# Earlier row gathers, stored up-products spread over all groups, and gates asked for mid-group in a product-key expert block

## The chip, the core and the metric

The kernel runs on one core of one Trainium2 chip. TensorE (PE) multiplies matrices into PSUM, VectorE (DVE) and ScalarE (ACT) work on SBUF and PSUM, GpSimd (POOL) issues the indirect gathers, SyncE (SP) issues most plain transfers, and 16 DMA engines carry out what all of them issue. The metric is the device time of one execution in microseconds.

## What is computed

One residual block on 512 tokens of width 2048, all in float32:

```
x = x + mixer(rms_norm(x))        # 8 stick-breaking and 8 forgetting heads, gated, projected
h = rms_norm(x)
x = x + peer_ffn(h)
out = rms_norm(x)

peer_ffn, for each token:
    for each of 8 heads: two 256-wide half queries score 128 sub-keys each,
        the best 16 of both sides are combined, and the best 16 of the 256 sums
        name 16 of 16384 experts, with softmax gates
    act  = gelu(dot(u[expert], h))             # 128 chosen experts a token
    out += gate * act * v[expert]
```

## The kernel before, in words

Every float32 operand of a matrix product is split into a rounded part and a rest, and a product is three matmuls (`mm3`, lines 115 to 118). `wload` (line 95) fetches a block of weights of 128 x 2048 in two halves of 512 KB through SP into `wr` (four buffers once `more` is set), ACT writes the rounded half `wh` (line 108) and DVE the rest `wl` (line 109). A block is 48 matmuls; in the expert part these have 352 columns.

**Two ways to the experts.** The first 352 tokens (`TD`) are computed densely: for each block c of 128 experts, of `NK` = 128 blocks, `expert_up(c)` multiplies by `uT[c]`, scales by `rstd` on DVE (line 536) and applies gelu on ACT; the product is multiplied by the gates of the block (zero where the token has not chosen the expert) and then by the block's rows of `vP`. The other 160 tokens (128 and 32) are done by gathering their rows: a queue `todo` of 325 items holds 128 + 32 gathers from `expert_u` and 128 + 32 from `expert_v` (one indirect DMA of 128 rows of 8 KB each on POOL, line 561, and one pass of DVE over 128 x 2048, lines 568, 577, 586, 597), and five entries for the changes of stage, two of them empty. `pace(after, units)` adds `units * rate[0]` to a counter and issues one item for each whole unit, its DVE pass placed behind the instruction `after`.

**The stages of the second half.** (1) Query: sixteen projections `wload(w_q[b])` with 512 columns, and after each pair `choose(h, ...)` for the last 256 tokens, some 70 small DVE instructions. After all heads one instruction writes `idx`, the 128 chosen rows of each of the last 128 tokens (line 741). (2) Early: `choose` for the first 256 tokens, and after each head `early(UPS, pace)`, which computes five up-products and stores them in DRAM (`gact_sp`); then 22 steps (line 777) that write the gates of 16 tokens each to DRAM (`gsp`), with further up-products in between. In all `NS` = 54 up-products are stored. The rate is `SLOW` = 0.8 items for each up-product. (3) The loop over 16 groups of `GC` = 8 blocks. `weigh(n)` makes sure that block n + 1 (`LEAD` = 1) is there too, by `fetch`: a stored product is read back (`gl<-gact_sp`, 176 KB, line 802), any other is computed. At the first block of a group it asks for the gates of the whole group in three transfers (`h<-gsp`, lines 812 to 815, pieces of 512 bytes, into one buffer `gg` in the unused columns of `h2`), multiplies (line 817), and splits into `wg` (lines 820 and 821). There are four buffers `gl` and nine `wg`. With the group's eight `wg` in place, eight blocks of `vP` are multiplied into `psy` and added to `acc` (line 841). An up-product and a `vP` block are one unit of the pace each; on entry to the loop the rate becomes the items left over 2 * 128 - 54 - 8 = 194.

In the kernel before, the stored products are blocks 0 to 53, so groups 0 to 5 and most of group 6 compute no up-product in the loop, and the later groups compute all eight. The order on each engine is laid out by a planner when the program is built, from program order, readiness and its own estimate of times; each engine then runs its list in order, waiting where data are not there.

Of the kernel before, what the change touches and what calls it, by code (L numbers as in the profile page):

```python
# [13 lines left out]
ALU = mybir.AluOpType  # L14
# [6 lines left out]
NT = T // P  # L21
D = 2048
KC = D // P
HD = 128
NH = 8
NK = 128
TOPK = 16
HK = NH * TOPK
# [3 lines left out]
GC = 8  # L32
NG = NK // GC
JJ = D // (GC * P)
TB = 16
# [3 lines left out]
TD = T - P - MB  # L39
# [2 lines left out]
CW = 112  # L42
UPS = 5
NS = NH * UPS + TD // TB - -(-(TD // TB) // 3)
SLOW = 0.8
LEAD = 1
NP = 4
# [3 lines left out]
def block_kernel(ctx, tc, xT, gains, w_vf, bf, w_qk, w_v, w_g, w_br, w_o, w_q, keysT, uT, vP, expert_u, expert_v, outT):  # L51
    nc = tc.nc
# [39 lines left out]

    WC = D // 2 + 4 * NH

    def wload(src, between=None, pace=None):

        out = []
        n = src.shape[-1] // 2
        for s in range(2):
            turn[0] += 1  # L100
            rp = more[0] if more and turn[0] % 2 else wp
            raw = rp.tile([P, WC], F32, tag="wr", name="wr", bufs=2)[:, :n]
            nc.sync.dma_start(raw, src[:, s * n:(s + 1) * n])
            if between and s == 0:
                between()
            hi = wp.tile([P, WC], F32R, tag="wh", bufs=3, name="wh")[:, :n]
            lo = wp.tile([P, WC], F32R, tag="wl", bufs=3, name="wl")[:, :n]
            nc.scalar.activation(hi, raw, AF.Copy)  # L108
            ins = nc.vector.tensor_tensor(lo, raw, hi.bitcast(F32), op=ALU.subtract)  # L109
            out.append((hi, lo))  # L110
            if pace and s == 0:
                pace(ins, 0.5)
        return out

    def mm3(ps, wh, wl, ah, al, start, stop):
        nc.tensor.matmul(ps, wh, ah, start=start, stop=False)  # L116
        nc.tensor.matmul(ps, wh, al, start=False, stop=False)  # L117
        nc.tensor.matmul(ps, wl, ah, start=False, stop=stop)  # L118

    def proj(ps, w, a, nk=KC, off=0, n=T):  # L120
        for k in range(nk):
            b = off + k
            wh, wl = w[b // 8]
            c = slice(b % 8 * P, (b % 8 + 1) * P)
            mm3(ps, wh[:, c], wl[:, c], a[:, k, 0, :n], a[:, k, 1, :n], k == 0, k == nk - 1)
# [12 lines left out]
    with ExitStack() as s1:  # L138
# [3 lines left out]
        with ExitStack() as s2:  # L142
# [16 lines left out]

            xload(0, 1)  # L160
            firstw = wload(w_qk[0, 0, 0], lambda: xload(1, 1))
            for k in range(2, KC, 2):
                xload(k, 2)
            for k in range(KC):
# [3 lines left out]
                                               op1=ALU.subtract)  # L168
# [252 lines left out]
            ps = pa.tile([P, NT, NH], F32, tag="z1", name="psc")  # L421
# [5 lines left out]
            ps = pa.tile([P, T], F32, tag="z0", name="pscT")  # L427
# [34 lines left out]
        h2 = h2p.tile([P, KC, 2, T], F32R, name="h2")  # L462
        with ExitStack() as s2:
# [7 lines left out]
            for j in range(KC):  # L471
                ps = pp.tile([P, T], F32, tag="pp", name="pso")
# [5 lines left out]
                                               op1=ALU.subtract)  # L478
# [8 lines left out]
    gsp = dram.tile([P, TD // TB, NK, TB], F32, name="gsp")  # L487
# [6 lines left out]
    idx = gpool.tile([P, HK], U32, name="idx")  # L494
# [37 lines left out]
    def expert_up(c, pace=None):  # L532
        ps = pu.tile([P, T], F32, tag="pu", name="psu")
        proj(ps[:, :TD], wload(uT[c], pace=pace), h2, n=TD)
        g = gl.tile([P, TD], F32, tag="gl", name="gl")
        ins = nc.vector.tensor_tensor(g, ps[:, :TD], rstd[:, :TD], op=ALU.mult)  # L536
        if pace:
            pace(ins, 0.5)
        nc.scalar.activation(g, g, AF.Gelu_apprx_tanh)
        return g  # L540
# [3 lines left out]
    gg = h2.rearrange("p k s t -> p (k s) t")[:, :TD // TB, TD:TD + GC * TB].bitcast(F32)  # L544
    gg = gg.rearrange("p b (c t) -> p b c t", t=TB)
# [3 lines left out]
    def pace(after, units):  # L549

        slot[0] += units * rate[0]
        while todo and slot[0] >= 1:
            f, i = todo.pop(0)
            f(i, after.ins)
            slot[0] -= 1
# [57 lines left out]
    todo = [(gather_up, i) for i in range(HK)] + [(lambda i, after: None, 0), (rows_b, 0)]  # L613
    todo += [(gather_up_b, i) for i in range(SB)] + [(gather_down, i) for i in range(HK)]
    todo += [(gather_down_b, i) for i in range(SB)] + [(lambda i, after: None, 0), (back, 0), (back_b, 0)]
    rate = [SLOW]

    gact_sp = dram.tile([NS, P, TD], F32, name="gact_sp")
    started = []

    def early(n, pace=None):
        for _ in range(n):
            if len(started) < NS:
                c = len(started)
                nc.scalar.dma_start(gact_sp[c], expert_up(c, pace))
                started.append(c)

    with ExitStack() as s1:
# [6 lines left out]
        ia = s1p.tile([P, NT, HK], F32, name="ia")  # L635
        ib = s1p.tile([P, NT, HK], F32, name="ib")
# [77 lines left out]
                                    op=ALU.mult)  # L714


        for h in range(NH):
            sc = []
            sv = se.tile([P, 2, HT, NK], F32, tag="sv", name="sv")
            for p in range(2):  # L720
                b = 2 * h + p
                if b == 1:
                    norm2()
                if b == 3:
                    token_rows(lambda k: acc[:, k, T - P:], h2g, accg)
                ps = pu.tile([P, T], F32, tag="pu", name="psq2")
                proj(ps, wload(w_q[b]), h2)
                q = se.tile([P, T], F32, tag="ab1", name="q2")
                nc.scalar.activation(q, ps, AF.Copy)
                kt = se.tile([P, NK], F32, tag="kt", name="kt")  # L730
                nc.sync.dma_start(kt, keysT[b])
                ps = psx.tile([P, NT, NK], F32, tag="psx", name="pss")
                for t in range(NT):
                    nc.tensor.matmul(ps[:, t], q[:, t * P:(t + 1) * P], kt, start=True, stop=True)
                nc.scalar.activation(sv[:, p], ps[:, :HT], AF.Copy)
                sc.append(ps[:, HT:])
            nc.scalar.dma_start(scores[h], sv)
            choose(h, sc, HT, NT - HT)


        nc.vector.scalar_tensor_tensor(idx, ia[:, NT - 1], float(NK), ib[:, NT - 1], op0=ALU.mult, op1=ALU.add)
        nc.vector.tensor_copy(ggate, gt[:, NT - 1])
        rep = se.tile([P, 2 * HK + 2], F32, tag="ab1", name="rep")
        nc.vector.scalar_tensor_tensor(rep[:, :HK], ia[:, NT - 2], float(NK), ib[:, NT - 2], op0=ALU.mult, op1=ALU.add)
# [4 lines left out]
        ps = psx.tile([P, T], F32, tag="psx", name="psrep")  # L749
# [18 lines left out]
        for n, src in enumerate((ia, ib, gt)):  # L768
            ps = psx.tile([P, ND, P], F32, tag="psx", name="pstr")
# [7 lines left out]
        for tb in range(TD // TB):  # L777
            st = se.tile([P, NK, TB], F32, tag="st", name="st")
            for t4 in range(0, TB, 4):
# [4 lines left out]
                ps = pg.tile([P, 4, NK], F32, tag="pg", name="psgt")  # L784
                for i in range(4):
                    t = tb * TB + t4 + i
                    nc.vector.tensor_scalar(ab[0][:, i], i128, tr[0][:, t:t + 1], tr[2][:, t:t + 1], op0=ALU.is_equal,  # L787
                                            op1=ALU.mult)
# [7 lines left out]
    extra.append(ex)  # L796

    def fetch(c):
        if c >= NS:
            return expert_up(c, pace)  # L800
        g = gl.tile([P, TD], F32, tag="gl", name="gl")
        nc.sync.dma_start(g, gact_sp[c])
        return g


    ahead = []

    def weigh(n):

        while len(ahead) < min(n + 1 + LEAD, NK):  # L810
            ahead.append(fetch(len(ahead)))
        if n % GC == 0:
            for b in range(0, TD // TB, 8):
                e = min(b + 8, TD // TB)
                nc.sync.dma_start(gg[:, b:e], gsp[:, b:e, n:n + GC])
        g = ahead[n]
        nc.vector.tensor_tensor(g.rearrange("p (b t) -> p b t", t=TB), g.rearrange("p (b t) -> p b t", t=TB),
                                gg[:, :, n % GC], op=ALU.mult)
        wg = ex.tile([P, 2, TD], F32R, tag="wg", bufs=GC + 1, name="wg")
        nc.scalar.activation(wg[:, 0], g, AF.Copy)  # L820
        nc.vector.tensor_tensor(wg[:, 1], g, wg[:, 0].bitcast(F32), op=ALU.subtract)  # L821
        return wg

    ws = [weigh(0)]
    assert len(started) == NS
    rate[0] = len(todo) / (2 * NK - NS - 8)
    py2 = pool("py2", 2, space=PSUM)
    for grp in range(NG):
        while len(ws) < GC:
            ws.append(weigh(grp * GC + len(ws)))  # L830
        for jb in range(KC // JJ):
            w = wload(vP[grp, jb])
            for jj in range(JJ):
                j = jb * JJ + jj
                ps = (py, py2)[j % 2].tile([P, T], F32, tag="py", name="psy")
                for c in range(GC):
                    b = jj * GC + c
                    wh, wl = w[b // 8]
                    cc = slice(b % 8 * P, (b % 8 + 1) * P)
                    mm3(ps[:, :TD], wh[:, cc], wl[:, cc], ws[c][:, 0], ws[c][:, 1], c == 0, c == GC - 1)  # L840
                add = nc.vector.tensor_tensor(acc[:, j, :TD], acc[:, j, :TD], ps[:, :TD], op=ALU.add)
                pace(add, 1.0 / JJ)
        ws = []
    while todo:
        pace(add, 1.0)

# [14 lines left out]
    ps = pu.tile([P, NT, 2], F32, tag="pu", name="psn3")  # L861
# [65 lines left out]
```

## Time and profile before

| | |
|---|---|
| runs of the kernel before | 3780.71, 3785.07, 3790.12 us, median 3785.07 |
| the profiled execution, its own time | 3782.03 us |
| its span, first to last instruction | 3780.3 us |
| mean granted TensorE clock | 0.989 |
| busy: PE, DVE, ACT, POOL | 97%, 70%, 34%, 14% |
| bytes read from and written to HBM | 784.72 MB, 39.11 MB |

Times in the rows are microseconds from the span's start, "ns" where so marked. A matmul's duration overlaps that of the next, so a busy PE can still be below its best rate: the number of matmuls in a stretch tells that. "A <- B" is a wait of A for B.

### The profile page before, as it was taken

Reading aid. Unit: us, or ns where it says so; the run is one execution under the profiler, and the core shown is the slowest. Engines: PE = TensorE matmul, PEld = TensorE weight load, DVE = VectorE, ACT = ScalarE, POOL = GpSimd, SP = SyncE. Lnnn points to the kernel's source line nnn. Section 1 sums busy time; section 2 is a strip of 40 time slices with the busy share of each in tenths; the row PEclk is TensorE's granted clock in tenths of the full one; section 3 lists DMA queues with packets and bytes.
Section 4 is the critical chain, followed back from the end, with each engine's and each line's share of the span. In section 5 each row is a group of like instructions: output and inputs, shape, how many; then the busy total and the mean of one; then the engine's idle time right before and its main releaser. Section 6 shows DMA issues by size and latency. Waiting matters only on the chain.

```text
span 3780.3 us, 52236 instructions
## 1 busy us (share of the span) xinstructions
PE 3676.0 (97%) x20745; PEld 3384.4 (90%) x20745; DVE 2640.2 (70%) x4067; ACT 1291.3 (34%) x1808; POOL 515.2 (14%) x432
## 2 busy tenths in 40 slices
PE   8999999999999999999999898999999999999997
PEld 7888888888887878799999798999999999999997
DVE  5333445444555346799699888988888888888885
ACT  4334222232223223344355332333333333333333
POOL 0000000000000000011211122222222222222220
PEclk9999999999999999999999999999999999999999
DMA  4222222222224233376867899998999989999983
GB/s 141 80 78 77 98 95 95 89 87 84 85 95 138 95 100 101 128 267 251 294 229 264 288 336 333 352 334 326 333 336 348 345 324 349 340 343 344 332 306 112
DMA packets 233701, 827.26 MB, mean 219 GB/s; under 512 B 21736, under 2 KB 82664, under 8 KB 189680
## 3 DMA queue, kind: packets, MB, share of 16 engines
q1 hardware_dynamic: 174032, 450.30, 34.5%
q0 software_dynamic: 49920, 360.74, 24.8%
q10 hardware_dynamic: 9504, 12.88, 0.9%
q8 instruction: 163, 2.67, 0.3%
q14 instruction: 82, 0.67, 0.1%
HBM read 784.72 MB, written 39.11 MB: 218 GB/s over the span
## 4 chain that ended last, share of the span: by engine, by line
PE 81%; DVE 9%; DMA 5%; issue 3%; ACT 1%; SPq 0%; POOL 0%; DVEq 0%; POOLq 0%; ACTq 0%
PE psy L118 7%; PE psy L117 7%; PE psy L116 7%; PE psu L118 6%; PE psu L116 6%; PE psu L117 6%; PE psg L118 3%; PE psg L117 3%; PE psq L118 3%; PE psg L116 3%; PE psq L117 3%; PE psq L116 3%; DVE wl L109 2%; DVE ab L787 2%; PE psk L118 2%
## 5 line engine op out<-in xcount | busy, mean ns | idle before, releaser
L108 ACT ACTIVATE wh<-wr 128x1024 fp32r<-128x1024 f32 x768 | 813.6, 1061 | 1933.4 <-PE psy L117 581.0
L109 DVE TENSOR_TENSOR wl<-wr,wh 128x1024 fp32r<-128x1024 f32 x768 | 935.5, 1221 | 504.4 <-ACT wh L108 500.5
L116 PE MATMUL psy<-wg,wh 128*128 128x352 f32 x2048 | 668.6, 327 | 26.6 <-ACT wg L820 25.8
L117 PE MATMUL psy<-wg,wh 128*128 128x352 f32 x2048 | 672.0, 328 | 8.7 <-DVE wg L821 8.7
L118 PE MATMUL psu<-h,wl 128*128 128x352 f32 x2048 | 666.7, 326 | 12.8 <-DVE wl L109 12.5
L118 PE MATMUL psy<-wg,wl 128*128 128x352 f32 x2048 | 669.8, 328 | 8.4 <-DVE wl L109 8.3
L116 PE MATMUL psu<-h,wh 128*128 128x352 f32 x2048 | 666.6, 325 | 4.0 <-DVE gl L536 2.9
L117 PE MATMUL psu<-h,wh 128*128 128x352 f32 x2048 | 662.8, 324 | 0.0
L116 PEld LDWEIGHTS psy<-wg,wh 128*128 128x128 f32 x2048 | 391.1, 191 | 29.0 <-ACT wg L820 27.6
L118 PEld LDWEIGHTS psu<-h,wl 128*128 128x128 f32 x2048 | 385.5, 188 | 18.9 <-DVE wl L109 18.7
L117 PEld LDWEIGHTS psy<-wg,wh 128*128 128x128 f32 x2048 | 391.0, 191 | 11.0 <-DVE wg L821 10.9
L118 PEld LDWEIGHTS psy<-wg,wl 128*128 128x128 f32 x2048 | 391.0, 191 | 10.0 <-DVE wl L109 9.9
L116 PEld LDWEIGHTS psu<-h,wh 128*128 128x128 f32 x2048 | 386.6, 189 | 5.0 <-issue 3.2
L117 PEld LDWEIGHTS psu<-h,wh 128*128 128x128 f32 x2048 | 386.9, 189 | 0.0
L561 POOL DMA_INDIRECT row<-eu,idx x128 | 192.4, 1503 | 901.5 <-DVE row L568 606.4
L568 DVE SCALAR_TENSOR_TENSOR row<-row,rstd_t,h2g 128x2048 f32<-128x2048 f32 x128 | 300.1, 2345 | 6.5 <-DMA row<-eu,idx 6.5
L586 DVE SCALAR_TENSOR_TENSOR acc<-row,gact,acc 128x2048 f32<-128x2048 f32 x128 | 300.1, 2345 | 1.9 <-DMA row<-ev,idx 1.9
L561 POOL DMA_INDIRECT row<-ev,idx x128 | 182.2, 1424 | 508.0 <-DVE acc L586 478.1
L116 PE MATMUL psq<-h,wh 128*128 128x512 f32 x512 | 204.5, 399 | 8.8 <-ACT wh L108 8.8
L117 PE MATMUL psq<-h,wh 128*128 128x512 f32 x512 | 205.6, 401 | 1.5 <-DVE h L167 1.4
L118 PE MATMUL psq<-h,wl 128*128 128x512 f32 x512 | 204.6, 400 | 0.1
L118 PE MATMUL psg<-h,wl 128*128 128x512 f32 x512 | 203.3, 397 | 0.0
(311 smaller groups left out, 5513.7 us busy)
## 6 DMA issues: line engine op xcount, KB each, us to landing
wr<-uT SPq DMA_DIRECT2D x256, 512.0 KB
wr<-vP SPq DMA_DIRECT2D x256, 512.0 KB
wr<-w_qk SPq DMA_DIRECT2D x64, 512.0 KB
wr<-w_g SPq DMA_DIRECT2D x64, 512.0 KB
gsp<-st POOLq DMA_DIRECT2D x22, 1024.0 KB
wr<-w_br SPq DMA_DIRECT2D x32, 512.0 KB
wr<-w_o SPq DMA_DIRECT2D x32, 512.0 KB
wr<-w_q SPq DMA_DIRECT2D x32, 512.0 KB
```

The source lines that it names most:

```text
L108: nc.scalar.activation(hi, raw, AF.Copy)
L109: ins = nc.vector.tensor_tensor(lo, raw, hi.bitcast(F32), op=ALU.subtract)
L116: nc.tensor.matmul(ps, wh, ah, start=start, stop=False)
L117: nc.tensor.matmul(ps, wh, al, start=False, stop=False)
L118: nc.tensor.matmul(ps, wl, ah, start=False, stop=stop)
L561: nc.gpsimd.indirect_dma_start(out=row.rearrange("p k q -> p (k q)"), out_offset=None, in_=table, in_offset=bass.IndirectOffsetOnAxis(ap=i ...
L568: nc.vector.scalar_tensor_tensor(row, row, rstd_t[:, NT - 1:NT], h2g, op0=ALU.mult, op1=ALU.mult, accum_out=gact[:, i:i + 1])
L586: nc.vector.scalar_tensor_tensor(accg, row, gact[:, i:i + 1], accg, op0=ALU.mult, op1=ALU.add)
L787: nc.vector.tensor_scalar(ab[0][:, i], i128, tr[0][:, t:t + 1], tr[2][:, t:t + 1], op0=ALU.is_equal, op1=ALU.mult)
```

## The change

Three parts. **Rows:** `idx` is written head by head in the query stage, and from projection b = 5 on each half of a `w_q` block calls `qpace`, which issues gathers at `QROWS` = 0.75 items a call as long as fewer have been issued than are known; `rate` goes to `SLOW` after the query stage. **Spread:** the 54 stored products are no longer blocks 0 to 53 but the list `EARLY`, three or four in each group (2, 4, 7 in group 0; 9, 11, 14 in group 1; 16, 18, 21, 23 in group 2, and so on). **Gates:** `weigh` asks for no gates. `gates(grp)` is called for group 0 ahead of the loop, and for the next group behind the `vP` block jb = 1; behind block jb = 6 the next group's first block is weighed, into the ninth `wg`.

```diff
+EARLY = [c for c in range(NK) if (c + 1) * NS // NK > c * NS // NK]
+QROWS = 0.75
...
-    def wload(src, between=None, pace=None):
+    def wload(src, between=None, pace=None, both=False):
...
-            if pace and s == 0:
-                pace(ins, 0.5)
+            if pace and (both or s == 0):
+                pace(ins, 1.0 if both else 0.5)
...
-    rate = [SLOW]
+    rate = [QROWS]
...
-                c = len(started)
-                nc.scalar.dma_start(gact_sp[c], expert_up(c, pace))
+                c = EARLY[len(started)]
+                nc.scalar.dma_start(gact_sp[len(started)], expert_up(c, pace))
...
+        known = [0]
+
+        def qpace(after, units):
+
+            if HK - len([f for f, _ in todo if f is gather_up]) < known[0]:
+                pace(after, units)
+
         for h in range(NH):
...
-                proj(ps, wload(w_q[b]), h2)
+                proj(ps, wload(w_q[b], pace=qpace if b > 4 else None, both=True), h2)
...
             choose(h, sc, HT, NT - HT)
-
-
-        nc.vector.scalar_tensor_tensor(idx, ia[:, NT - 1], float(NK), ib[:, NT - 1], op0=ALU.mult, op1=ALU.add)
+            hk = slice(h * TOPK, (h + 1) * TOPK)
+            nc.vector.scalar_tensor_tensor(idx[:, hk], ia[:, NT - 1, hk], float(NK), ib[:, NT - 1, hk], op0=ALU.mult,
+                                           op1=ALU.add)
+            known[0] += TOPK
+
+
+        rate[0] = SLOW
...
     def fetch(c):
-        if c >= NS:
+        if c not in EARLY:
             return expert_up(c, pace)
         g = gl.tile([P, TD], F32, tag="gl", name="gl")
-        nc.sync.dma_start(g, gact_sp[c])
+        nc.sync.dma_start(g, gact_sp[EARLY.index(c)])
         return g
 
+    def gates(grp):
+        for b in range(0, TD // TB, 8):
+            e = min(b + 8, TD // TB)
+            nc.sync.dma_start(gg[:, b:e], gsp[:, b:e, grp * GC:(grp + 1) * GC])
...
-        if n % GC == 0:
-            for b in range(0, TD // TB, 8):
-                e = min(b + 8, TD // TB)
-                nc.sync.dma_start(gg[:, b:e], gsp[:, b:e, n:n + GC])
...
+    gates(0)
     ws = [weigh(0)]
...
     for grp in range(NG):
+        ahead_w = []
         while len(ws) < GC:
             ws.append(weigh(grp * GC + len(ws)))
         for jb in range(KC // JJ):
             w = wload(vP[grp, jb])
+            if grp + 1 < NG and jb == 1:
+                gates(grp + 1)
+            if grp + 1 < NG and jb == KC // JJ - 2:
+                ahead_w.append(weigh((grp + 1) * GC))
...
-        ws = []
+        ws = ahead_w
```

## Rows read from the trace of the kernel before

**Rows 1.** The page's parts 1 and 2: busy time, and DVE in 40 slices.

```profile
PE 3676.0 (97%) x20745; PEld 3384.4 (90%) x20745; DVE 2640.2 (70%) x4067; ACT 1291.3 (34%) x1808; POOL 515.2 (14%) x432
...
DVE  5333445444555346799699888988888888888885
```

**Rows 2.** Busy time by stretch, two slices of the loop's second half.

```profile
2835.00:2929.50 94.50, 94.50 (x588) 94.50 (x587) 81.96 (x74) 31.76 (x37) 24.63 (x18) 1.00 0.92 349
2929.50:3024.00 94.50, 94.50 (x587) 94.50 (x586) 81.02 (x71) 28.98 (x32) 26.24 (x17) 1.00 0.92 346
```

**Rows 3.** Busy time by stage: query, early, loop; columns as named in its first line.

```profile
core 0: us, PE busy (x) PEld busy (x) DVE busy (x) ACT busy (x) POOL busy (x), PEclk, DMA share, GB/s
1440.00:1580.00 140.00, 139.98 (x652) 113.90 (x652) 99.47 (x416) 47.06 (x111) 0.00 (x0) 1.00 0.32 103
...
1620.00:1900.00 280.00, 275.11 (x1703) 272.96 (x1702) 241.70 (x638) 124.06 (x200) 42.92 (x28) 1.00 0.75 268
2130.00:2585.00 455.00, 429.60 (x2552) 424.32 (x2553) 389.44 (x470) 138.09 (x166) 115.28 (x75) 0.96 0.92 335
2585.00:3685.00 1100.00, 1092.38 (x6749) 1089.22 (x6747) 947.87 (x894) 361.45 (x428) 286.77 (x199) 1.00 0.90 336
```

**Rows 4.** Busy time in short stretches of the loop, the group boundaries among them.

```profile
2120.00:2140.00 20.00, 8.99 (x39) 8.34 (x40) 7.84 (x17) 4.40 (x9) 0.99 (x1) 0.66 0.63 207
2140.00:2180.00 40.00, 40.00 (x249) 40.00 (x248) 37.86 (x44) 11.65 (x12) 12.00 (x8) 1.00 0.94 337
2180.00:2220.00 40.00, 35.37 (x199) 34.37 (x198) 30.83 (x38) 11.53 (x15) 10.05 (x7) 0.91 0.91 321
2260.00:2280.00 20.00, 16.30 (x92) 16.01 (x91) 14.96 (x21) 6.42 (x11) 2.62 (x2) 0.91 0.97 343
2320.00:2360.00 40.00, 33.49 (x187) 32.54 (x186) 29.93 (x38) 10.88 (x15) 7.02 (x5) 0.87 0.89 312
2400.00:2440.00 40.00, 37.05 (x227) 36.36 (x226) 36.38 (x47) 12.99 (x17) 9.55 (x7) 1.00 0.99 366
2460.00:2500.00 40.00, 35.37 (x198) 34.55 (x198) 32.50 (x41) 12.29 (x17) 9.16 (x7) 0.91 0.94 334
2580.00:2600.00 20.00, 18.90 (x115) 18.32 (x114) 17.71 (x19) 5.82 (x7) 5.04 (x3) 1.00 0.75 273
2700.00:2740.00 40.00, 40.00 (x249) 40.00 (x248) 34.16 (x37) 11.12 (x11) 11.77 (x7) 1.00 0.94 356
3080.00:3100.00 20.00, 17.06 (x96) 16.76 (x95) 15.45 (x15) 5.26 (x6) 4.53 (x3) 0.91 0.73 273
3320.00:3340.00 20.00, 18.22 (x112) 17.93 (x111) 13.33 (x13) 5.92 (x7) 3.36 (x2) 1.00 0.81 287
3580.00:3600.00 20.00, 17.42 (x98) 17.12 (x98) 13.49 (x12) 4.52 (x5) 4.13 (x3) 0.91 0.77 278
```

**Rows 5.** Chain of waits from 1600 us to the end: start, length, what.

```profile
1674.54 7.75 DMA row<-eu,idx
...
2119.43 5.83 DMA gsp<-st
2125.38 3.65 DMA h<-gsp
...
2195.53 7.20 DMA gl<-gact_sp
...
2756.30 8.96 DMA row<-eu,idx_b
...
3070.27 14.16 DMA h<-gsp
```

**Rows 6.** Waits from 2120 to 2620 us: total, times, longest.

```profile
DVE gl L817 <- DMA gl<-gact_sp: 21.9, 10, 4.4
DVE gl L817 <- DMA h<-gsp: 18.1, 2, 11.3
```

**Rows 7.** The same from 2620 to 3700 us.

```profile
DVE gl L817 <- DMA h<-gsp: 31.4, 7, 8.8
```

**Rows 8.** Waits of the query stage, 1440 to 1580 us.

```profile
DVE wl L109 <- ACT wh L108: 34.4, 12, 4.4
```

**Rows 9.** The page's part 5: the DVE pass over one gathered row.

```profile
L568 DVE SCALAR_TENSOR_TENSOR row<-row,rstd_t,h2g 128x2048 f32<-128x2048 f32 x128 | 300.1, 2345 | 6.5 <-DMA row<-eu,idx 6.5
```

## Prediction

> **What bounds the kernel now.** I read the page's shares first: TensorE is busy 97% of the span, VectorE 70%, but VectorE's slices show that this mean hides a second half at mostly eight or nine tenths [rows 1]. A busy PE is no measure of its rate, so next I looked for a stretch where nothing holds it. Two slices of the loop have 588 and 587 matmuls in 94.5 us [rows 2], 0.1607 us each; 20 us then hold 124.5 matmuls and 40 us 249. With that yardstick the loop was cut into stretches of 20 us, and the reader is to see that PE runs at its best rate everywhere except at group boundaries [rows 4]. The chain of waits and the waits by pair say what is late there: either a stored product (`gl<-gact_sp`, 7.20 us in the chain) or the gates (`h<-gsp`, 14.16 us) [rows 5, 6, 7]. In the query stage VectorE has 99.5 of 140 us taken and PE loses nothing [rows 3]. So PE's work sets the end, and only what PE loses can be won.
>
> **What there is to win.** (a) Five boundaries in the part with all products stored: 199, 92, 187, 227 and 198 matmuls where 249, 124.5, 249, 249 and 249 fit [rows 4]: 217.5 missing, times 0.1607 = 35.0 us. The cause can be read from the buffers: when a group ends, four products lie in `gl`, the other four must be read back with nothing for PE to do, and the stretch's mean granted clock falls to 0.87 at the lowest [rows 4], a part of it being spent at the lower of the two levels (1.2 of 2.4 GHz) after the gap, which the count includes. (b) Four boundaries further on: 115, 96, 112 and 98 where 124.5 fit [rows 4]: 77 missing, 12.4 us. Here VectorE stood waiting for the gates, 31.4 us in seven waits [rows 7], with the remainders `wl` of the weights behind it in its queue; PE's stock of split weights covers part of each. (c) The entry to the loop: 39 instead of 124.5 between 2120 and 2140 us [rows 4], 13.7 us: the last write of `gsp` takes 5.83 us to land, the gates read from it 3.65 us [rows 5], and PE has no other work. Sum 61.1 us. As a cross-check, the two stages of the loop hold 2552 + 6749 = 9301 matmuls in 1555 us [rows 3], where 9676 fit: 60 us, of which the first lies partly in (c) and some are transposes. So about 61 us is the whole prize; the change can't win more, except by lightening VectorE.
>
> **The change part by part.**
>
> *Spread and gates, loop.* The work is the same: 54 products read, 74 computed, 48 matmuls each. In place of boundaries with eight loads there are now boundaries with three or four loads and four or five up-products, so at least four times 48 x 0.1607 = 7.71 us of PE work, 31 us, lies across a boundary; a load in the chain took 7.20 us, and two in a row fit. A boundary of this kind does not exist before. The nearest rows: in the later part, with eight up-products across each boundary, some boundaries lose nothing (249 of 249 between 2700 and 2740 us), the smallest loss among those listed is that of 2580 to 2600 us, 9.5 matmuls or 1.5 us [rows 4]. Where the group's last block is computed and the next one is stored, PE has only the first seven blocks' 21 matmuls, 3.4 us, to cover the last one's chain of scale, gelu, gates and split. So each of the 15 boundaries costs between 0 and 1.5 us; I take 0.5 (the later rows are nearer), 7.5 in all, bounds 0 and 22. The gates of the next group are asked for behind block jb = 1 and first used behind jb = 6, five blocks or 38 us later, against the 14.16 us that the slowest transfer took [rows 5]: (b) goes. Their three transfers stand on SP ahead of the weights of jb = 2; four `wr` buffers, two blocks or 15.4 us of PE, hide them, and without that cover it is what they took beyond it, nothing at 14.16 us. The ninth `wg` is free from the group before, so the early `weigh` waits for nothing. What is late next is the last `wg` of a group, the cost counted above.
>
> *Entry.* `gates(0)` stands on SP ahead of the weights of up-products 0 and 1, which need neither gates nor `gsp`. Two blocks of weights fit in `wr` while the last scatter runs; they are 15.4 us of PE for a gap of 13.7. If SP is held at the last gates transfer before those weights are asked for, most of the gap stays. Bounds: 0 and 13.7 kept; the weights of the loop's first blocks were loaded early before too, so I keep 3.
>
> *Rows in the query stage.* From b = 5, 22 half blocks call the pace: 22 x 0.75 = 16.5, so 16 gathers. Never more than known: 32 are known at b = 5. Each costs VectorE 2.345 us [rows 9], 37.5 us in all; the seven more index writes are a microsecond together. The stage from 1440 us has 99.5 of 140 us taken [rows 3]; 137 to 138 would be. This is the tight place: of VectorE's idle time 34.4 us are waits for `wh` [rows 8], which itself waits for PE to release a buffer, so they come where VectorE is ahead of PE, and a row behind the `wl` just uses the time before the next. Lower bound 0; upper bound 37.5, all of it on the path. The nearest row is the early stage, VectorE at 241.7 of 280 and for most of it near full: 1703 matmuls where 1742 fit, 6.3 us lost [rows 3]. I take 6. POOL is idle in this stretch (0.00) and DMA at 0.32 [rows 3], so the gathers themselves have room.
>
> *Rate.* Before, 43 items are issued in the early stage at 0.8, and 325 - 43 = 282 are left: 282/194 = 1.45 a unit. After, 61 are gone (16 in the query stage, 43, and two in the first `weigh`): 264/194 = 1.36. VectorE gains 0.09 x 2.4 = 0.2 us on each unit of 7.71 us. Worth 0 as PE is not held by it between boundaries [rows 2]; at most a few microseconds below the sum. The end of the queue stays about 8 units ahead of the loop's, so the tail is as before.
>
> *Transfers.* A mean group after has 8 + 4.6 units, 97.3 us: 12.6 weight blocks and 17.2 rows of 1.05 MB, 1.44 MB of gates, 0.6 MB of products: 33.3 MB, 343 GB/s. The loop ran at PE's best rate with 349 and 346 [rows 2], so this costs nothing. The Trainium skill's page "DMA: Bandwidth & Descriptors", section "Specifications", gives about 358 GB/s of HBM for a core; by that the group would need 93 us, still under PE's 97.
>
> **Sum.** 61.1 - 7.5 (boundaries) - 3 (entry) - 6 (query) = 44.6 us. The profiled execution took 3782.03, so 3737.4; the median of the runs lies 3 us above it, 3785.07, so 3740.5. I say 3739.
>
> **The rivals.**
>
> *VectorE fills up in the query stage.* The extra passes delay `wl` or `choose`, and the chain at the end (`idx`, then the small matmul that spreads it, in order on PE) starts that much later. Speaks for it: 137 of 140 us. Against: the early stage lost 6.3 us at a like load. At the upper bound the gain is 61.1 - 10.5 - 37.5 = 13: 3772; halfway 3755. It decides when more than 30 of the 37.5 us reach PE.
>
> *Gathers starved.* VectorE's long instructions hold up POOL's gathers, and each row's pass waits in VectorE's queue. If each of 16 comes late by one pass of 2.345 us, the price is again 37.5 us: 3772. Against it: gathers landed in 7.75 us in the early stage and 8.96 us in the loop [rows 5], no sign of it. The Trainium skill's "SBUF — State Buffer", section "SBUF: two separate sides", has such a rule: an instruction of VectorE that takes both ports locks GpSimd out of writing descriptors, 620 ns grown to 3100; an estimate by it is 16 x 2.5 = 40 us. The 7.75 us bear that out for none of these instruction kinds.
>
> *Loads stall VectorE (slower).* In mixed groups each stored product is weighed in order on VectorE; if its load comes late, everything behind waits, `wl` too. Over the 1557 us of PE work in the loop VectorE has 14% free by the later stage's 947.87 of 1100 [rows 3], 218 us, or 4.0 us for each of 54 loads; beyond it each microsecond costs 54. It eats the gain at 4.9 us a load; at 5.5 us, 297 - 218 = 79 us of loss give 3820. For it: waits of up to 4.4 us now, 7.20 us in the chain. Against: the ten waits mean 2.2 us [rows 6], and these are the loads with nothing ahead of them.
>
> *DMA as the bound.* If the loop can move only the 336 GB/s of its later stage [rows 3], 16 groups of 33.3 MB take 1586 us instead of 1557: 29 of the 44.6 us go back, 3769. Against: 349 and 346 at full PE rate.
>
> *The index writes wait.* If the planner treats `idx` as one tile, each of the six later writes waits on VectorE for gathers in flight that read it, some 8.96 us: 54 us where 3 are free, so 3741 + 51 = 3792, and the rows part does not do what it says. The slices are disjoint, which speaks against.
>
> **How the numbers follow.** Forecast 0.64; VectorE full 0.15; starved 0.02; loads stall 0.06; DMA 0.08; index writes 0.05. The forecast alone spans 3715 (61 us and some lightness of VectorE) to 3755. The range reaches up to 3772, the upper bound of the query cost, which takes in VectorE full and most of DMA; the stalling loads and the index writes stay outside, with some of the forecast's edges. From no change, this kernel's measurement can tell about 0.3%, 11 us. Faster is the forecast, nearly all of VectorE full (to 3772) and most of DMA: 0.82; same 0.09, from the ends of those two and some index writes; slower 0.09, the loads and the rest of the index writes.
>
> **What would show it.** Stored products: the waits of `gl` for `gact_sp` near nothing, and stretches at group boundaries, now every 97 us, with 245 or more of 249 matmuls. Gates: no `h<-gsp` in the chain after the first group. Entry: `psu` matmuls between the last scatter and the first `psy`. Query: 16 passes of line 568 before the early stage, and the last `psq` matmul not more than 6 us later. Wrong it would be if `wl` waits grow in the query stage, if `gl` waits for loads sum to more than 200 us, or if the loop has fewer than 580 matmuls in a typical 94.5 us away from boundaries.

## The result and the profile after

The change makes the kernel slower: 3807.28 us (3799.6 to 3813.42, five runs) against 3785.07 us (3780.71 to 3790.12, five runs), a ratio of 1.0054 with a 95% interval of 1.0035 to 1.0073. The forecast of 3739 us and its range are missed on the upper side. The profiled execution took 3813.42 us, at the upper end of its runs.

Its milestones, the starts of the last matmuls of each kind, say in which stage. The last `psq` matmul comes at 1579.8 us (1577.1 before), the last gate matmul `psgt` at 2123.1 (2117.7), the last `psy` at 3787.9 (3757.8). So the stages ahead of the loop cost 5.4 us, and the loop, from the last `psgt` to the last `psy`, takes 1664.8 us where it took 1640.1: 24.7 of the 30 us are lost where the forecast saw the gain.

The page's parts 1 and 2 of the kernel after [rows 1]:

```profile
PE 3692.1 (97%) x20745; PEld 3391.3 (89%) x20745; DVE 2639.5 (69%) x4074; ACT 1291.3 (34%) x1810; POOL 547.3 (14%) x432
...
DVE  5333454434555459999699787887878888788885
```

The busy time by stage, columns as in [rows 3]:

```profile
1440.00:1580.00 140.00, 138.56 (x634) 111.46 (x633) 132.41 (x452) 44.77 (x109) 23.83 (x16) 1.00 0.61 220
1620.00:1900.00 280.00, 272.24 (x1666) 269.63 (x1665) 240.20 (x641) 123.81 (x198) 44.13 (x28) 0.99 0.73 262
2130.00:2585.00 455.00, 433.03 (x2578) 428.02 (x2577) 359.26 (x422) 139.84 (x170) 101.28 (x70) 0.96 0.84 307
2585.00:3685.00 1100.00, 1067.51 (x6503) 1056.31 (x6502) 913.75 (x882) 345.38 (x407) 303.04 (x185) 0.99 0.89 326
```

The query stage did what was forecast: 16 gathers on POOL, VectorE at 132.4 of 140 us, PE hardly hurt. The loop did not. Its long second stage now has 6503 matmuls where it had 6749, and VectorE is *less* busy there, 913.75 instead of 947.87 us. So VectorE did not run out of time; it stood.

The same in stretches of 20 us [rows 4], a selection:

```profile
2120.00:2140.00 20.00, 20.00 (x131) 19.86 (x131) 8.95 (x17) 7.36 (x10) 1.53 (x2) 1.00 0.87 313
2140.00:2160.00 20.00, 13.38 (x67) 12.54 (x66) 17.64 (x22) 7.34 (x11) 4.60 (x4) 0.88 0.66 240
2160.00:2180.00 20.00, 20.00 (x120) 20.00 (x120) 17.55 (x23) 7.75 (x11) 3.63 (x3) 0.95 0.84 309
...
2280.00:2300.00 20.00, 16.87 (x89) 16.57 (x90) 16.61 (x21) 5.74 (x7) 4.34 (x3) 0.83 0.87 304
...
2820.00:2840.00 20.00, 17.67 (x100) 17.37 (x99) 18.88 (x17) 6.15 (x6) 6.71 (x4) 0.91 0.82 312
```

A free stretch holds 124.5. Counting every such stretch from 2120 us up to the last `psy` with fewer than 121 matmuls, the kernel before has 13 of them with 61.0 us missing, the kernel after 26 with 80.2. The losses did not go; they became smaller and twice as many, one or two at each boundary.

Who waits is in the waits of VectorE of the kernel after, 2120 to 2620 us and then 2620 to 3700 us (total, times, longest; before in [rows 6, 7]):

```profile
DVE gl L830 <- DMA h<-gsp: 15.6, 3, 7.2
...
DVE gl L830 <- DMA gl<-gact_sp: 12.2, 4, 4.2
...
DVE gl L830 <- DMA gl<-gact_sp: 52.6, 16, 5.9
...
DVE gl L830 <- DMA h<-gsp: 24.7, 5, 8.9
```

and in those of PE over the loop, 2120 to 3700 us. Before:

```profile
PE psy L116 <- ACT wg L820: 25.8, 6, 12.1
PE psy L117 <- DVE wg L821: 8.7, 5, 3.6
PE psy L118 <- DVE wl L109: 8.3, 4, 2.9
PE psu L118 <- DVE wl L109: 0.9, 1, 0.9
```

After:

```profile
PE psu L120 <- DVE wl L111: 26.7, 15, 3.3
PE psy L120 <- DVE wl L111: 15.2, 9, 2.8
PE psy L118 <- ACT wg L833: 7.3, 4, 3.1
...
PE psy L119 <- DVE wg L834: 1.4, 2, 0.8
```

PE used to wait for a group's weighed products (`wg`, 34.5 us); the change removes most of that (8.7 us are left). In its place PE waits for `wl`, the rest of *any* weight block, 41.9 us where it was 9.2. And `wl` is late because VectorE stands in front of a stored product or of the gates: 70.1 us in 23 waits and 40.3 us in 8 over the whole span, against 21.9 and 49.5 before. All waits of PE in this window grow from 44.5 to 53.9 us, 9.4 of the 24.7 us that the loop is longer; the count of missing matmuls, which takes in those that run slower after a gap, gives 19.2, and some 5 us lie in stretches that miss only a few matmuls and were not followed.

One boundary in the timeline, with start, duration, instruction and, in brackets, the idle time before it and what ended it:

```profile
2266.80 0.33 SPq L105 DMA_DIRECT2D wr<-vP  x1
2267.18 0.45 SPq L815 DMA_DIRECT2D gl<-gact_sp  x1
...
2272.06 0.53 DVE L830 TENSOR_TENSOR gl<-gl,h 128x352 f32<-128x352 f32 x1
2276.74 0.53 DVE L830 TENSOR_TENSOR gl<-gl,h 128x352 f32<-128x352 f32 x1 [4.15 <-DMA gl<-gact_sp]
2277.18 1.18 DVE L834 TENSOR_TENSOR wg<-gl,wg 128x352 fp32r<-128x352 f32 x2
2278.78 1.23 DVE L111 TENSOR_TENSOR wl<-wr,wh 128x1024 fp32r<-128x1024 f32 x1 [0.42 <-ACT wh L110]
...
2280.06 0.43 PE L120 MATMUL psy<-wg,wl 128*128 128x352 f32 x1 [0.67 <-DVE wl L111]
2280.33 0.32 PE L118 MATMUL psy<-wg,wh 128*128 128x352 f32 x1
2280.35 2.34 DVE L570 SCALAR_TENSOR_TENSOR row<-row,rstd_t,h2g 128x2048 f32<-128x2048 f32 x1
...
2283.72 0.66 PE L118 MATMUL psy<-wg,wh 128*128 128x352 f32 x1 [3.08 <-ACT wg L833]
2284.18 0.49 PE L119 MATMUL psy<-wg,wh 128*128 128x352 f32 x1
2284.48 0.49 PE L120 MATMUL psy<-wg,wl 128*128 128x352 f32 x1
```

The load is asked for at 2267.18, right behind a transfer of weights in SP's list, and is there at 2276.7, 9.6 us later. VectorE reaches its multiplication 4.15 us too soon and stands; the `wl` and the rest of the group's `wg` come that much later, and PE loses 0.67 and 3.08 us. A pass over a gathered row (2280.35, 2.34 us) stands between that `wl` and the group's last product and is a part of the 3.08; no run takes these passes out of the boundaries. After the gap matmuls start 0.29 to 0.30 us apart instead of 0.16, the lower of TensorE's two levels, until 2288.3 (the stretch's mean granted clock is 0.83): another 2 us or so. Together 5.7 us, the 35.5 matmuls that are missing in this stretch.

It is not the `gl` buffer that the request waits for. All 54 requests go out 0.04 to 0.05 us behind a transfer of weights in SP's list, and the profile names no wait of SP for any of them. What SP waits for is the weights' own buffers, which come free with `wl` (2120 to 3700 us; the first line is of the kernel after, the second of the kernel before, whose requests did wait for `gl`):

```profile
SPq L105 <- DVE wl L111: 1237.7, 349, 10.3
...
SPq L802 <- DVE wg L821: 34.1, 22, 5.1
```

The request at 2267.18 needs the buffer of the block four before, whose last reader ended at 2260.46; for every request but the first that reader ended at least 6.7 us earlier. From the request to the multiplication pass 8.0 us at the median, while a load took 6.6 us at the median and up to 12.2. So the load is late because it is asked for one weighing ahead and stands behind weights in SP's list.

The gates: at 2800.38 SP issues the three transfers for the next group, early as the change wants it. But the first weighing of the next group is laid out too early as well:

```profile
2800.38 7.63 SPq L821 DMA_DIRECT2D h<-gsp  x3
...
2818.51 0.53 DVE L830 TENSOR_TENSOR gl<-gl,h 128x352 f32<-128x352 f32 x1 [6.59 <-DMA h<-gsp]
...
2820.47 2.35 DVE L588 SCALAR_TENSOR_TENSOR acc<-row,gact,acc 128x2048 f32<-128x2048 f32 x1
2822.74 1.22 DVE L111 TENSOR_TENSOR wl<-wr,wh 128x1024 fp32r<-128x1024 f32 x1
...
2824.01 0.43 PE L120 MATMUL psy<-wg,wl 128*128 128x352 f32 x1 [2.33 <-DVE wl L111]
```

In the program it stands behind block jb = 6; on VectorE it came some 18 us after the request, in the middle of the group, with the more urgent `wl` behind it. The chain of waits [rows 5] has this transfer and a load:

```profile
2780.17 6.65 DMA gl<-gact_sp
...
2804.60 13.79 DMA h<-gsp
```

### The profile page after: what moved, and what is told of

Same layout as the page of the kernel before. It is cut to its first block, busy times and chain, and to the rows that moved or that the text cites. A ratio compares the mean times of both kernels' runs of the same rounds, so it can differ in the third digit from the quotient of the medians.

```text
span 3811.7 us, 52171 instructions
## 1 busy us (share of the span) xinstructions
PE 3692.1 (97%) x20745; PEld 3391.3 (89%) x20745; DVE 2639.5 (69%) x4074; ACT 1291.3 (34%) x1810; POOL 547.3 (14%) x432
## 5 line engine op out<-in xcount | busy, mean ns | idle before, releaser
L120 PE MATMUL psy<-wg,wl 128*128 128x352 f32 x2048 | 670.5, 328 | 15.2 <-DVE wl L111 15.2
L118 PEld LDWEIGHTS psu<-h,wh 128*128 128x128 f32 x2048 | 390.6, 191 | 11.4 <-issue 8.7
L119 PEld LDWEIGHTS psu<-h,wh 128*128 128x128 f32 x2048 | 390.8, 191 | 0.0
L570 DVE SCALAR_TENSOR_TENSOR row<-row,rstd_t,h2g 128x2048 f32<-128x2048 f32 x128 | 300.3, 2346 | 26.7 <-DMA row<-eu,idx 26.5
L563 POOL DMA_INDIRECT row<-ev,idx x128 | 215.0, 1679 | 549.5 <-DVE acc L588 526.3
```

The costliest lines, as they stand in the source:

```text
L563: nc.gpsimd.indirect_dma_start(out=row.rearrange("p k q -> p (k q)"), out_offset=None, in_=table, in_offset=bass.IndirectOffsetOnAxis(ap=i ...
L570: nc.vector.scalar_tensor_tensor(row, row, rstd_t[:, NT - 1:NT], h2g, op0=ALU.mult, op1=ALU.mult, accum_out=gact[:, i:i + 1])
```

## The experiments

The theory (L): a stored product is asked for only inside the boundary, so it is late; VectorE works in order, and whatever stands behind the wait, `wl` above all, is late with it. When the experiments were laid out, L also held that the request waits for a free `gl` buffer. Rivals: the gates are what is late (G); the rows part has moved work to where it hurts (R); the loop is simply short of DMA or of VectorE time (D); in the expectations from e5 on, V is the part of D that VectorE has more to do at a mixed boundary than PE's time covers. All ratios are against the kernel before on the same chip, with 95% intervals; its median was 3782.7 us beside e1 to e4, 3784.95 beside e5 to e8 and 3790.18 beside e9 to e12, so ratios can be compared throughout, and times only within these sets. All differences are under 2%. The loop is from the last `psgt` to the last `psy` of the profiled execution; the last two columns are the waits of `gl` on VectorE, us and times.

| kernel | us | ratio | loop | loads | gates |
|---|---|---|---|---|---|
| before | 3785.07 | 1 | 1640.1 | 21.9, 10 | 49.5, 9 |
| after | 3807.28 | 1.0054 [1.0035, 1.0073] | 1664.8 | 70.1, 23 | 40.3, 8 |
| e1_rows | 3800.96 | 1.0048 [1.0031, 1.0066] | 1646.0 | 17.4, 6 | 55.8, 8 |
| e2_spread | 3829.5 | 1.0126 [1.0105, 1.0146] | 1687.4 | 70.8, 24 | 47.9, 9 |
| e3_gates | 3788.21 | 1.0012 [1.0003, 1.0022] | 1651.1 | 26.1, 10 | 29.8, 6 |
| e4_spread_gates | 3803.43 | 1.0054 [1.0037, 1.0071] | 1674.3 | 59.4, 20 | 45.1, 8 |
| e5_no_loads | 3747.84 | 0.9904 [0.9884, 0.9924] | 1597.7 | none | 9.9, 3 |
| e6_pin | 3787.77 | 1.0002 [0.9991, 1.0013] | 1638.2 | 65.5, 27 | 7.0, 1 |
| e7_own | 3747.85 | 0.9907 [0.9886, 0.9929] | 1598.0 | none | 13.8, 4 |
| e8_own_pin | 3749.49 | 0.9906 [0.9886, 0.9925] | 1599.3 | none | 6.5, 1 |
| e9_own_norows | 3752.73 | 0.9903 [0.9883, 0.9922] | 1610.4 | none | 5.4, 3 |
| e10_own_nogates | 3759.92 | 0.9926 [0.9908, 0.9945] | 1608.1 | 7.6, 1 | 35.4, 8 |
| e11_lead2 | 3792.89 | 1.0015 [1.0003, 1.0028] | 1641.8 | 54.5, 22 | 57.0, 10 |
| e12_own_unspread | 3784.9 | 0.9991 [0.9978, 1.0004] | 1643.6 | 21.7, 11 | 47.7, 7 |

**The parts alone.** e1_rows is the kernel before with the query stage's gathers alone:

```diff
...
-                proj(ps, wload(w_q[b]), h2)
+                proj(ps, wload(w_q[b], pace=qpace if b > 4 else None, both=True), h2)
...
```

> Only the rows part: idx written head by head, 16 gathers issued in the query stage at 0.75 a half block; stored products and gates as before. Theory L (the loads of stored products, now between computed blocks, are waited for in order on VectorE): this part costs only what the stages before the loop lost in the changed kernel, 3 to 6 us, and gives back as much in the loop: 3780 to 3792, same as before. Rival G (the early weighing waits for the gates): the same, 3780 to 3792. Rival R (the gathers in the query stage are the cost): slower by most of the 22 us, 3800 or more.

e2_spread has only the choice of the stored blocks:

```diff
...
-                c = len(started)
+                c = EARLY[len(started)]
...
-        if c >= NS:
+        if c not in EARLY:
...
```

> Only the list EARLY: 54 stored products spread over all groups; gathers and gates as before. Theory L: slower than before, 3795 to 3815, with 15 or more waits of VectorE for gl<-gact_sp, 50 us or more in all, against 10 waits of 21.9 us before. Rival G: faster than before, 3735 to 3770, since the boundaries without computed blocks are gone and no block is weighed early. Rival R: faster likewise, 3735 to 3770.

e3_gates has only `gates(grp)`, asked for at jb = 1, and the weighing ahead:

```diff
...
+            if grp + 1 < NG and jb == 1:
+                gates(grp + 1)
+            if grp + 1 < NG and jb == KC // JJ - 2:
+                ahead_w.append(weigh((grp + 1) * GC))
...
```

> Only the gates part: next group's gates asked for behind the block jb = 1, its first block weighed behind jb = 6; stored products 0 to 53 and gathers as before. Theory L: within 10 us of before either way, 3775 to 3795; the waits for h<-gsp change place and not their sum, some 40 to 50 us. Rival G: slower by most of the 22 us, 3800 or more. Rival R: 3770 to 3785.

e4_spread_gates has these two and not the rows part.

> Spread and gates together, gathers as before. Theory L: as the whole change within 8 us, 3798 to 3815, with the waits for gl<-gact_sp at some 70 us. Rival G: as the whole change too, 3798 to 3815, but then e3 is slow and e2 is not. Rival R: 3735 to 3785, as the gathers are where they were.

Spreading alone costs 1.26%, 48 us, and brings the same waits for loads as the whole change (70.8 and 70.1 us). With the gates part it costs 0.54%, so that part takes 27 us back; alone it is near nothing (+0.12%). The rows part alone costs 0.48%, 18 us, though its profiled execution, at the low end of its runs, shows only 11; added to the other two it changes nothing that can be measured (e4 against the whole change). VectorE's products in e2 stand another 23.8 us, in three waits, for which the profile names no cause.

Not every expectation held. e1 fell into R's range (3800 us or more) and not into L's (3780 to 3792); e2 is slower than L's 3795 to 3815; in e3 VectorE waits 29.8 us for gates where L had 40 to 50, in e4 59.4 us for loads where it had some 70. What speaks against R is that e2 and e4, with the gathers where they were, are slower than before, where R had 3735 to 3770 and 3735 to 3785. So spreading is what costs in the change, and the 18 us of e1 stay without an explanation.

**The loads.** e5_no_loads is the whole change without reading the stored products back; VectorE multiplies the gates by another tile in their place, so the sums are not those of the reference:

```diff
-        g = gl.tile([P, TD], F32, tag="gl", name="gl")
-        nc.sync.dma_start(g, gact_sp[EARLY.index(c)])
-        return g
+        return None
...
+        if g is None:
+            g, src = gl.tile([P, TD], F32, tag="gl", name="gl"), rstd[:, :TD]
...
```

> The whole change, but the stored products are not read back: VectorE multiplies the gates by a tile that is there already in their place, as many instructions as before; what is left out is the reading of 54 products, so the sums are not those of the reference. Theory L (VectorE's waits for late loads, 70 us in 23 waits, hold back the remainders of the weights): 3745 to 3780, 30 to 60 us under the whole change, and the waits of PE for wl fall from 56 us to under 25. Rival V (VectorE has more to do at a mixed boundary than PE's time, 7.4 of 7.7 us for a computed block and over 1 us for each stored one without any matmul): 3795 to 3810, hardly moved. Rival G (gates): 3795 to 3810.

e6_pin is the whole change with the weighing ahead held behind the last addition of block jb = 5:

```diff
-                ahead_w.append(weigh((grp + 1) * GC))
+                while len(ahead) < (grp + 1) * GC + 1 + LEAD:
+                    ahead.append(fetch(len(ahead)))
+                with tc.issue_after(add.ins):
+                    ahead_w.append(weigh((grp + 1) * GC))
```

> The whole change, and the weighing of the next group's first block held behind the last addition of block jb = 5 on VectorE, where the program text has it, so that the planner can't move it up. Theory L: only the waits for h<-gsp inside the groups go, 25 to 40 us of VectorE, part of which PE had covered: 3785 to 3803. Rival G: 3765 to 3785. Rival V: 3795 to 3810.

e7_own is the whole change with places of their own for the stored products of one group, in columns of `h2` that lie unused. All of a group's products are asked for together with its gates, during the group before, and VectorE multiplies from there into `gl`, in two instructions because the place is in two pieces:

```diff
...
+    def ask(grp):
+        for i, c in enumerate([c for c in EARLY if c // GC == grp]):
+            big, small = flat[:, 22 + 2 * i:24 + 2 * i, TD:], flat[:, 30, TD + 32 * i:TD + 32 * (i + 1)]
+            src = gact_sp[EARLY.index(c)]
+            nc.sync.dma_start(big, src[:, :320].rearrange("p (r t) -> p r t", r=2))
+            nc.sync.dma_start(small, src[:, 320:])
+            stash[c] = (big, small)
...
                 gates(grp + 1)
+                ask(grp + 1)
```

> The whole change, with four places of their own for the stored products in unused columns of h2, asked for together with the next group's gates instead of one block ahead; product and gates are multiplied into gl in two instructions. Theory L: as in e5, 3745 to 3785, with next to no waits for gact_sp. Rival V: 3795 to 3815, as VectorE has one more short instruction for each product. Rival G: 3795 to 3810.

e8_own_pin has both.

> e6 and e7 together. Theory L: the lowest of these, 3730 to 3770, below the kernel before. Rival V: 3790 to 3810. Rival G: as e6 within 10 us.

This settles that late loads are the cost. Without the loads the loop takes 1597.7 us; with all of them, asked for about 100 us ahead of their use, 1598.0. So it is neither their bytes nor their instructions that cost, only their lateness. (PE's waits for `wl` over the whole span fall from 55.9 to 26.6 us in e5, where under 25 was expected.) Both are 0.9% faster than the kernel before and some 1.5% faster than the change. The stages of e7_own, columns as before, and the longest of the waits of PE in its loop by total, where the change has 26.7 and 15.2 us:

```profile
2130.00:2585.00 455.00, 443.27 (x2708) 438.40 (x2707) 379.94 (x462) 148.41 (x181) 102.21 (x74) 0.99 0.89 323
2585.00:3685.00 1100.00, 1097.75 (x6780) 1091.00 (x6779) 941.87 (x950) 364.62 (x434) 278.17 (x185) 1.00 0.90 331
```

```profile
PE psu L120 <- DVE wl L111: 11.8, 9, 3.8
```

6780 matmuls where 6845 fit, with VectorE at 941.87 us and DMA at 331 GB/s, both more than in the slower kernel: D falls, and V with it. The passes over gathered rows are still there. Five stretches of 20 us have fewer than 121 matmuls, 15.7 us in all, the worst two being the entry and one boundary where VectorE stood 3.84 us for a gathered row:

```profile
2140.00:2160.00 20.00, 16.02 (x87) 15.16 (x86) 17.20 (x22) 6.93 (x11) 5.30 (x4) 0.91 0.62 237
...
2320.00:2340.00 20.00, 16.23 (x91) 15.94 (x90) 11.44 (x15) 5.02 (x6) 4.30 (x3) 0.91 0.70 255
```

One more rival can be read from the traces: that requests standing in SP's list hold up the weights behind them. ScalarE's waits for weights, 2120 to 3700 us, after and then e7_own:

```profile
ACT wh L110 <- DMA wr<-vP: 33.0, 14, 6.5
...
ACT wh L110 <- DMA wr<-vP: 92.1, 30, 7.8
```

The kernel before has 40.9 us of them in 19 waits, so the change has fewer than it, and the faster kernel the most: late weights are not what the change loses by.

Holding the early weighing back (e6) removes most of the waits for gates (40.3 to 7.0 us) and is worth 20 us while the loads are late; with the loads in time it is worth nothing (e8). G is a part of the loss, not an independent one. With it held back, the change is level with the kernel before (1.0002), its 65.5 us of waits for loads notwithstanding: the late loads take the gain away, and the late gates beside them make it a loss. In ratios: both in time (e8) 0.9906; late gates alone (e10, below) 0.9926; late loads alone (e6) 1.0002; both late (e2, without the rows part) 1.0126.

**What the other parts are worth then.** e9_own_norows is e7_own without the rows part; e10_own_nogates is e7_own with the gates asked for at the group's first weighing and none made ahead (both undo the hunks shown for e1 and e3).

> Spread, gates and own places for the stored products, without the gathers of the query stage. If the rows part is only its 5 us ahead of the loop (last psgt near 2118 instead of 2124, and the loop no longer than the 1598 us that the whole change with own places takes): 3740 to 3746. If earlier gathers leave VectorE and POOL freer in the loop, so that the rows part pays for itself: a loop of 1603 us or more and 3747 to 3765. The four-stage loss of the change itself (loads waited for) is gone in either case: no gl waits for gact_sp above 5 us in sum.

> Rows, spread and own places; the gates are asked for at the group's first weighing, as in the kernel before, and no weighing is made ahead. If the two waits, for loads and for gates, are separate costs, the gates part is worth here what it was worth on top of the spreading alone (3829.5 to 3803.4, 26 us): 3765 to 3780, with gl waiting for gsp at 6 boundaries for 40 us or more. If a boundary that no longer waits for loads has up-products enough to cover the gates: 3746 to 3758.

The rows part: 0.9903 without, 0.9907 with it, no difference. Its terms show in the profiles: with it the early stage ends 4.9 us later (2124.1 against 2119.2), and the loop is 12 us shorter (one profiled execution of each, on two chips). The second expectation, that it pays for itself, fits the loop. The gates part: 0.9926 without and 0.9907 with it, 7 us, with intervals that overlap; less than the 26 us that separate costs would give. The rival with 3746 to 3758 us is nearer to the 3759.9.

e11_lead2 is the change with one step more of lead and the same four buffers; e12_own_unspread the kernel before with own places for the first four stored products of each group:

```diff
-LEAD = 1
+LEAD = 2
```

> The change with blocks asked for two weighings ahead instead of one, with the same four gl buffers. If the lateness is that a gl buffer comes free only inside the boundary, asking earlier in the program changes little: waits of gl for gact_sp above 50 us in sum and 3790 to 3815. If one step of lead is all that was missing: waits under 25 us and 3750 to 3775.

```diff
     def fetch(c):
         if c >= NS:
             return expert_up(c, pace)
+        if c % GC < 4:
+            return None
...
```

> The kernel before with blocks 0 to 53 stored as it had them, and the first four of each stored group asked for a group ahead in own places; gates as before. If the late loads are a part of the boundaries of before as well, and spreading only adds to them: waits of gl for gact_sp under 8 us (21.9 before) and 3760 to 3775. If the boundaries of before are bound by PE having no other work (all products stored, nothing for PE to do but wait for the weighing) or by the gates: 3780 to 3788, and only the spreading with own places gives the gain.

The lead takes 15.6 of the 70.1 us of waits away and gets 0.4% back, where e7 gets 1.5%. The longest wait for a load is still 6.2 us (5.9 in the change), and the gates come later for VectorE than they did; the waits of its loop, 2120 to 3700 us:

```profile
DVE gl L830 <- DMA h<-gsp: 57.0, 10, 11.4
DVE gl L830 <- DMA gl<-gact_sp: 53.1, 21, 6.2
```

Time and waits came where L, with its buffer, had them (3790 to 3815 us, above 50 us), but the trace gives another reason: 50 of the 54 requests again stand right behind a transfer of weights in SP's list, and from request to multiplication pass 8.6 us at the median, 0.6 more than in the change. So one step earlier in the program is hardly earlier in time. e12 is no clean test: the other four products of each group are still asked for inside the boundary, and the waits for loads stay (21.7 us, where under 8 was the condition). What it shows is that, with all eight products stored, PE waits for the weighing itself as before, here over the loop:

```profile
PE psy L116 <- ACT wg L843: 23.3, 6, 12.1
PE psy L117 <- DVE wg L844: 11.4, 5, 4.6
```

Spreading *with* early loads (e10, which has the rows part too, 0.9926) gains over it; spreading without them (e2) loses more than anything else here.

## Why the prediction was wrong

**What bounds the kernel, and the prize: right.** PE sets the end, and the 61 us at the boundaries were there to be won: e7_own wins 42.1 us of loop and gives 6.4 back ahead of it, 35 us by the ratio, against the forecast's 44.6.

**The step that failed** is the cost of a mixed boundary: "each of the 15 boundaries costs between 0 and 1.5 us; I take 0.5", which rests on "at least four times 48 x 0.1607 = 7.71 us of PE work, 31 us, lies across a boundary; a load in the chain took 7.20 us, and two in a row fit". Leaving out the entry's 10.0 us (the stretches at 2140 and 2160), 80.2 - 10.0 = 70.2 us are missing after, 4.7 us for each of 15 boundaries, three times the upper bound. The 31 us of PE work are real but cannot be used as cover: one in three of those matmuls needs a `wl` that VectorE must still make, the others stand behind it in PE's order, and VectorE stands at the load. That the load would be asked for in time was taken without a reason: "two in a row fit" sets two loads against all 31 us, while the requests went out 8.0 us ahead of their use at the median. What covers a wait is only what VectorE has finished for PE before it stands, and in the boundary shown a wait of 4.15 us left PE short by 3.75. The rows chosen as nearest (boundaries with eight computed products) had no load in them.

**The rival "loads stall VectorE"** was the mechanism, at a chance of 0.06, and its price was wrong in the same way. It set waits against VectorE's spare 218 us in the loop, so that 4.9 us a load would eat the gain. Measured are 70.1 us for 54 loads, 1.3 us each, and the gain was gone and 20 us more (late gates among the cause, as e6 shows). Mean spare time is no allowance where the wait falls in the one place at which PE has no stock. The sign for being wrong, waits of more than 200 us, was too high by the same error.

**The gates:** half right. (b) "goes" if they are asked for at jb = 1 and first used behind jb = 6; the request came as forecast, but in the group shown the first use came 18 us after it and not 38, while the transfer took 13.79 us from the last issue on. Not foreseen was that the weighing offered early is put early into VectorE's list. e6 shows that it cost 20 us while the loads were late.

**Entry:** forecast as 3 us lost, bounds 0 and 13.7. Between 2120 and 2180 us there are 131 + 67 + 120 matmuls of 373.5: 8.9 us lost, where [rows 4] have 13.7. The up-products do come in first, as forecast, but VectorE then stands 6.74 us for the gates, and behind that two gaps of PE, 2.13 and 3.19 us, are waits for a `wl` that stands behind passes over gathered rows; one of these waited 2.36 us for its row.

**Query stage:** the term of 6 us and its sign were right: 16 gathers, the last `psq` 2.7 us and the last `psgt` 5.4 us later, and with and without the rows part 4.9 us (e7 and e9). VectorE filling up beyond that, starved gathers and waiting index writes did not come about: the sixteen gathers landed in 5.3 to 10.2 us, 8.0 at the median, and VectorE waited for none of them in this stage.

**Transfers:** right. e7_own runs its later stage at 99% of PE's best rate with 331 GB/s.

## What to carry to other kernels

Cover for a wait of an in-order engine is what that engine has already handed on, not the work that still needs it: look at what stands behind the waiting instruction before you count the other engine's work as cover. Moving loads into more places multiplies such waits unless each is asked for well ahead; here asking a group ahead, into four places of 176 KB, turned a loss of 0.5% into a gain of 0.9%. When a request goes out is read from the issuing engine's list, from what stands ahead of it there, and not from its place in the program. Work that is offered early to a planner may also be placed early, so an early request needs its first use held back as well.

## What the runs showed of the hardware

A small load was not quick beside heavy traffic here. Of the stored products (176 KB each) and the gates in the kernel after, the issues and, below each, the time from issue to landing, minimum, median and maximum:

```profile
L815 SPq DMA_DIRECT2D gl<-gact_sp x54: 422/426/1029, 2133.7 to 3719.5; - x54
...
DMA to landing us min/median/max: 3.2/6.6/12.2
...
L821 SPq DMA_DIRECT2D h<-gsp x48: 377/584/5731, 1992.9 to 3628.6; - x48
...
DMA to landing us min/median/max: 5.5/9.3/13.8
```

At about 326 GB/s the load takes 6.6 us at the median and up to 12.2. The Trainium skill's page "DMA: Bandwidth & Descriptors", section "Anatomy of one DMA — SWDGE (gpsimd) path", fits the time of a transfer issued from GpSimd by 2.0 us and its bytes at 436 GB/s; an estimate by it is 2.4 us for 176 KB. These transfers are issued from SP beside others, and no run here shows one without the traffic.

What stays open: why the rows part alone costs 18 us and nothing beside the other two; why the requests stand where they do in SP's list, and whether asking a group ahead would do without places of its own; and how far the kernel before would gain if all eight products of a group had places of their own, where e12 had four.
